# Ending a two-layer hybrid step: a third output tile beside the last recurrence, a listed order, sums on ScalarE, and a rotary product read from PSUM

## The chip, the cores and the metric

The kernel runs on one core of a Trainium2 chip. A core has a matmul engine (TensorE, PE in the profile, its weight loads PEld) and three engines that work on vectors: VectorE (DVE), ScalarE (ACT) and GpSimd (POOL); SyncE (SP) issues transfers. All work on a shared on-chip memory (SBUF); matmul results land in PSUM, eight banks of 512 fp32 columns on 128 partitions. The metric is the device time of one execution in microseconds (us), the median of several runs.

## The reference

The program is one step of a two-layer model of width 1024 on 640 tokens: 512 latent and 128 context tokens, five tiles of 128 tokens. Each layer modulates its input by an adaptive shift and scale, mixes tokens, multiplies by SiLU of a gate path, projects by an output weight, adds 4^0.25 times the residual, and normalises (LayerNorm). Layer 0 mixes by grouped-query attention with RMS-normalised queries and keys and rotary positions, layer 1 by a gated linear recurrence in both directions, eight heads of 128.

```python
q = _rms_norm(q.reshape(B, L, N_HEADS, HEAD_DIM), q_gain)     # layer 0
q = _apply_rope(q, cos, sin)          # xf * cos + rotated * sin
...
o = (o_fw + flip(o_bw)).transpose(0, 2, 1, 3)                 # layer 1
o = _rms_norm(o, norm_gain).reshape(B, L, REC_VAL_WIDTH)
gated = (o * jax.nn.silu(g.astype(jnp.float32))).astype(h.dtype)
return gated @ w_out, s_fw, s_bw
...
y = (xf - mu) * lax.rsqrt(var + LN_EPS) * g + b               # LayerNorm of x * alpha + gate * mixed
```

Outputs are both token streams, the new keys and values of the context tokens, and the final recurrent states (new_s).

## The kernel before

Each fp32 product is made of three matmuls of a shorter type: an operand is split in a high part (`hi`, a cast on ScalarE) and the rest (`lo`, a subtraction on VectorE or GpSimd), and hi x hi, hi x lo, lo x hi are added up in PSUM. The weights arrive in pieces of 512 KB (tile `raw`, SP's queue) and are split by `split_piece`.

The first half (layer 0 up to its output weights) stands in a block whose instructions a scheduler orders by an estimate of times. There, beside the attention of one group of heads (`att_gen`: scores `sc`, probabilities `p`, their transposes `pt`, and products `pot`), `q_gen` projects the queries of the next group in three units of tokens (two tiles, two tiles, one context tile): matmuls `qmm` into a bank, squares on ScalarE and their sums on VectorE, `rs_t` and a power on GpSimd (`rstd`), then on VectorE `qn` = bank x rstd, the rotary products `u` and `r` (for the context tile only the gain `qg`), the split into `qs2`, and four transposes `qps` on TensorE. Matmuls `adaps` for the adaptive gates stand between; VectorE adds them to `acc`.

The second half is written in program order. `proj_gen` projects one head (`vgps`, `rps`), 48 us each, while `gla_gen` works on the recurrence of the head before. A recurrence has seven levels: matmuls `lv` on TensorE, and products on the tile `A` on VectorE, with `kc` a copy on ScalarE. Then come transposes `kp`, their copy `kt`, the state products `sp`, six state updates and copies of the new state `ns`, the outputs `op`, squares of them on ScalarE (`ss`), `rs_t`, the power, the products with the norm and the gate (`on`), transposes `oT`, and their split `ghi`, `glo`. A `Lane` starts each stage of a recurrence when a counted time since the last is over.

The last head's recurrence has no projection beside it. `tail_gen` gives it other work: splitting the eight pieces of the output weight, and the output projection of token tiles 0 and 1 for heads 0 to 6 (slices k of the weight), 42 matmuls per tile. `weave` takes SIDE_T = 2.2 steps of it for each stage of the recurrence, and the tile framework places them. After the recurrence the five output tiles are finished one by one: the rest of the matmuls (`out_mms`, into `outp`, which has two banks), and `Norm(1, tt)`: per half `y` = outp x gate, `y` + alpha x, BN_STATS; then BN_AGGR, `rs_t`, power, and the closing pair of products with the norm's gain and bias, and the output's transfer, its halves on SP's and ScalarE's queues. Four PSUM tiles of two banks each serve all of this (`bank2`). The residual `x` comes from `x1a` by transfers on GpSimd's queue.

## Time and profile before

| | us |
|---|---|
| median of 3 runs | 873.47 (872.31 to 873.93) |
| the profiled execution | 873.58 |
| its span, first to last instruction | 871.8 |
| TensorE busy | 819.8 (94%) |
| VectorE busy | 533.8 (61%) |
| ScalarE busy | 373.0 (43%) |
| GpSimd busy | 212.9 (24%) |

The profile is of one execution. A row of its timeline has the start in us from the span's start, the length, engine, line and operation, output and inputs, the shape, and in brackets how long the engine stood idle ahead of it and which instruction ended that. Matmuls overlap, so the distance between two starts tells their cost, and a length does not. The granted clock is the share of TensorE's full clock.

### The profile page before, as it was taken

The numbers are of one execution on the slowest core, as the hardware profiler recorded it, in microseconds if no ns is written. First come the engines' busy times: TensorE is split into PE (matmuls) and PEld (weight loads), VectorE is DVE, ScalarE is ACT, GpSimd is POOL, SyncE is SP. The second block draws the span as 40 slices with busy tenths as digits, with TensorE's granted clock in tenths as the row PEclk, the third lists the DMA queues.
The fourth block names the chain that finished last, engine by engine and source line by source line (L and its number), as shares of the span: only waits on it lengthen the run. The fifth ranks groups of instructions, "written<-read, shape, count | busy, mean of one in ns | idle before, by whom it ended". The sixth has DMA issues, their size and how long they took to land.

```text
span 871.8 us, 19257 instructions
## 1 busy us (share of the span) xinstructions
PE 819.8 (94%) x8120; PEld 732.0 (84%) x8120; DVE 533.8 (61%) x952; ACT 373.0 (43%) x735; POOL 212.9 (24%) x263
## 2 busy tenths in 40 slices
PE   6999999979899988999999999999999999979794
PEld 4789998858778766888899999999999999977683
DVE  3656435735746666676437575758577576757485
ACT  2232536544655767222434444345354443453100
POOL 0213002533424644110001314042333243211010
PEclk9999999989999999999999999999999999989998
DMA  9932212162232253631223323332323232241131
GB/s 339 356 98 85 79 44 74 50 211 87 73 128 67 79 172 120 217 121 40 94 71 72 104 60 88 77 105 68 110 59 114 67 94 84 81 182 50 55 121 48
DMA packets 33991, 92.50 MB, mean 106 GB/s; under 512 B 5025, under 2 KB 12209, under 8 KB 33905
## 3 DMA queue, kind: packets, MB, share of 16 engines
q1 hardware_dynamic: 22416, 71.90, 24.5%
q0 software_dynamic: 4864, 14.44, 5.5%
q10 hardware_dynamic: 6624, 4.93, 1.9%
q8 instruction: 64, 1.05, 0.5%
q14 instruction: 23, 0.18, 0.1%
HBM read 82.06 MB, written 9.19 MB: 105 GB/s over the span
## 4 chain that ended last, share of the span: by engine, by line
PE 85%; DVE 5%; DMA 3%; ACT 3%; issue 1%; POOL 1%; SPq 0%; DVEq 0%; ACTq 0%; POOLq 0%
PE rps L1116 7%; PE rps L1117 6%; PE rps L1118 6%; PE vgps L1106 5%; PE vgps L1108 4%; PE vgps L1107 4%; PE outp L1001 4%; PE outp L1002 4%; PE outp L1003 4%; PE pot L758 3%; PE pt L840 3%; PE lv L1246 2%; PE gps L327 2%; PE gps L328 2%; PE gps L329 2%; PE sc L731 2%
## 5 line engine op out<-in xcount | busy, mean ns | idle before, releaser
L1116 PE MATMUL rps<-h1hi,rhi 128*128 128x320 f32 x368 | 117.9, 320 | 0.0
L1117 PE MATMUL rps<-h1lo,rhi 128*128 128x320 f32 x368 | 113.7, 309 | 0.0
L1118 PE MATMUL rps<-h1hi,rlo 128*128 128x320 f32 x368 | 113.5, 309 | 0.0
L833 POOL TENSOR_SCALAR p<-p,rc 128x640 f32<-128x640 f32 x64 | 54.6, 858 | 70.7 <-DVE rc L832 61.3
L1116 PEld LDWEIGHTS rps<-h1hi,rhi 128*128 128x128 f32 x368 | 69.1, 188 | 1.3
L1117 PEld LDWEIGHTS rps<-h1lo,rhi 128*128 128x128 f32 x368 | 69.2, 188 | 0.0
L1118 PEld LDWEIGHTS rps<-h1hi,rlo 128*128 128x128 f32 x368 | 69.1, 188 | 0.0
L222 DVE TENSOR_TENSOR rlo<-raw,rhi 128x1024 fp32r<-128x1024 f32 x32 | 45.0, 1410 | 33.9 <-ACT rhi L221 33.9
L1274 POOL COPY At<-near 32x160 f32<-32x160 f32 x32 | 14.0, 438 | 201.3 <-DVE near L1236 200.3
L828 ACT ACTIVATE p<-sc,nm 128x640 f32<-128x640 f32 x64 | 51.0, 798 | 24.8 <-DVE nm L825 21.0
L825 DVE TENSOR_REDUCE nm<-sc 128x1 f32<-128x640 f32 x64 | 51.8, 818 | 15.5 <-PE sc L732 15.2
L1224 ACT COPY kc<-A 128x640 f32<-128x640 f32 x40 | 32.2, 804 | 57.7 <-DVE A L1255 51.1
L221 ACT CAST rhi<-raw 128x1024 fp32r<-128x1024 f32 x32 | 33.6, 1049 | 49.9 <-PE rps L1117 47.0
L1106 PE MATMUL vgps<-rhi,h1hi 128*128 128x256 f32 x180 | 51.5, 286 | 1.2 <-ACT h1hi L956 1.2
L840 PE MATMUL pt<-small,p 128*128 128x128 f32 x320 | 50.2, 280 | 2.2 <-DVE acc L316 1.4
L1108 PE MATMUL vgps<-rhi,h1lo 128*128 128x256 f32 x180 | 50.8, 282 | 0.4 <-DVE h1lo L957 0.4
L1107 PE MATMUL vgps<-rlo,h1hi 128*128 128x256 f32 x180 | 50.6, 281 | 0.0
L736 ACT COPY pts<-pt 128x512 f32<-128x512 f32 x64 | 36.2, 589 | 32.9 <-PE pt L840 32.5
L731 PE MATMUL sc<-kk,X 128*128 128x320 f32 x128 | 42.5, 341 | 4.7 <-ACT p L828 4.2
L840 PEld LDWEIGHTS pt<-small,p 128*128 128x128 f32 x320 | 37.1, 142 | 11.2 <-issue 6.2
L1106 PE MATMUL vgps<-wspare,h1hi 128*128 128x256 f32 x140 | 41.6, 297 | 0.0
L327 PE MATMUL gps<-hhi,whi 128*128 128x320 f32 x128 | 40.0, 312 | 0.4 <-ACT X L584 0.4
(265 smaller groups left out, 2373.2 us busy)
## 6 DMA issues: line engine op xcount, KB each, us to landing
raw<-in_rec_w_in SPq DMA_DIRECT2D x40, 512.0 KB, 3.8
raw<-in_ada_s SPq DMA_DIRECT2D x32, 512.0 KB, 3.8
raw<-in_ada_m SPq DMA_DIRECT2D x16, 512.0 KB, 7.7
raw<-in_attn_w_in SPq DMA_DIRECT2D x16, 512.0 KB, 4.3
raw<-in_attn_w_out SPq DMA_DIRECT2D x8, 512.0 KB, 4.2
raw<-in_rec_w_out SPq DMA_DIRECT2D x8, 512.0 KB, 3.5
x1d<-y SPq DMA_DIRECT2D x5, 512.0 KB, 2.6
rx<-x1d POOLq DMA_DIRECT2D x20, 128.0 KB, 3.7
```

Of the source, the lines that this page charges most:

```text
L327: nc.tensor.matmul(ps[:, :320], w.hi(k)[:, c], hhi[:, k, t], start=(k == 0), stop=False)
L731: nc.tensor.matmul(out, X[:, h, t0:t0 + P], kk[:, c, k0:k1], start=True, stop=False)
L825: nc.vector.tensor_reduce(nm[:, 0:1], sc[:, :, :320], AX.XY, ALU.max, negate=True)
L828: nc.scalar.activation(halves(p[:]), sc[:, :, :320], AF.Exp, bias=nm[:, 0:1], accum_out=su[:, 0:1])
L833: nc.gpsimd.tensor_scalar(p, p, rs[:, 0:1], 1.0, ALU.mult, ALU.mult)
L840: nc.tensor.transpose(pt[:, i * 256 + q * P:i * 256 + (q + 1) * P], ps[q][:, (k0 + i) * P:(k0 + i + 1) * P], ident)
L1106: nc.tensor.matmul(out, h1hi[:, k, t], hi, start=(k == 0), stop=False)
L1107: nc.tensor.matmul(out, h1hi[:, k, t], lo, start=False, stop=False)
L1108: nc.tensor.matmul(out, h1lo[:, k, t], hi, start=False, stop=(k == KT - 1))
L1116: nc.tensor.matmul(ps[:, j, :320], hi[:, k, :], h1hi[:, k, t], start=(k == 0), stop=False)
L1117: nc.tensor.matmul(ps[:, j, :320], hi[:, k, :], h1lo[:, k, t], start=False, stop=False)
L1118: nc.tensor.matmul(ps[:, j, :320], lo[:, k, :], h1hi[:, k, t], start=False, stop=(k == KT - 1))
```

## The change

It has six parts.

1. Norm's sums on ScalarE. For layer 1, class `Norm` gives way to `Out`. For token tiles 0, 1, 3 and 2, in this order, BN_STATS and BN_AGGR go; ScalarE takes a sum of each half of `y` by a Copy with accumulation, and a sum of squares about the mean by a Square with accumulation: 16 new instructions on 128x512. VectorE works out the mean with two tiny operations (`spread`). Token tile 4, the last, keeps BN_STATS, in parts of 256 columns. Its second half is multiplied in two parts of 256 columns, 24 matmuls each.
2. Listed order. `tail_steps` gives out its steps one for each stage of the last recurrence; `weave` and `Side` are not used there. It goes on to the third output tile: slices 0 to 6 of tile 2, 42 matmuls, behind the levels, kp, sp and op.
3. Three pieces of the output weight (`wo_early`) are split during the last head's projection, one more than was there so far, into a new buffer `wx0`. Two of the five residual tiles are loaded early, the others after the last oT.
4. Gate ahead of norm: in `gla_gen`, `on` = op x g, then on x rstd, for every head. The squares' own output goes to `kt`, no longer to `on`.
5. Queries' rotary: `rope_raw` makes `u` and `r` from the bank before rstd is there, and `rms_scale` multiplies by rstd after. The count of operations is the same.
6. The transfers of four output tiles go on SP's queue alone.

```diff
@@ class Out (new), its statistics
+            for nh, s, y in todo:
+                nc.vector.scalar_tensor_tensor(y, self.x[:, s], ALPHA, y, ALU.mult, ALU.add)
+                if self.last:
+                    for i in range(s.start, s.stop, CW):
+                        nc.vector.bn_stats(self.st[:, self.n, :], self.y[:, i:i + CW])
+                        self.n += 1
+                else:
+                    j = junk.tile([P, 512], F32, tag="j", name="j")
+                    nc.scalar.activation(j, y, AF.Copy, accum_out=self.st[:, nh, 0:1])
...
+        def spread(self):
+            t = self.st
+            nc.vector.tensor_scalar(t[:, 0, 1:2], t[:, 0, 0:1], t[:, 1, 0:1], -1.0 / D, ALU.add, ALU.mult)
+            nc.vector.tensor_scalar(t[:, 0, 2:3], t[:, 0, 1:2], D ** -0.5, 0.0, ALU.mult, ALU.add)
+            for nh in range(2):
+                j = junk.tile([P, 512], F32, tag="j", name="j")
+                nc.scalar.activation(j, self.y[:, nh * 512:(nh + 1) * 512], AF.Square, bias=t[:, 0, 2:3], scale=D ** -0.5,
+                                     accum_out=t[:, 1, 1 + nh:2 + nh])
@@ q_gen
             ps = yield from tok_unit(w, tt0, n, "qmm")
             rstd = rms_stat(ps, n)
+            r = rope_raw(ps, tt0, n, cosq, sinq, qg)
             yield
...
-            qn = rms_apply(ps, n, rstd)
-            r = rope_apply(qn, tt0, n, cosq, sinq, qg)
+            qn = rms_scale(r, n, rstd)
@@ proj_gen
         for i in range(3):
             if i:
                 load_q(i)
+            if i == 2 and h == RH - 1:
+                wo_early()
@@ gla_gen
-            nc.scalar.activation(on[:, cc], opw[:, cc], AF.Square, accum_out=ss[:, c:c + 1])
+            nc.scalar.activation(kt[:, cc], opw[:, cc], AF.Square, accum_out=ss[:, c:c + 1])
+        nc.vector.tensor_tensor(on, opw[:, :NT], g, ALU.mult)
         rsqrt(rstd[:, :TT], ss[:, :TT], 1.0 / P, NORM_EPS)
...
-        nc.vector.tensor_tensor(on, on, g, ALU.mult)
+        on3 = on[:].rearrange("p (a b) -> p a b", a=TT)
+        nc.vector.tensor_tensor(on3, on3, view(rstd, 0, [[1, TT], [0, P]]), ALU.mult)
@@ the tail
+    def tail_steps():
+        slots.extend(wr.tile([P, 1024], F32R, tag=t, name=t)[:] for t in ("whi", "wlo"))
+        wo_piece(3)
         for tt in range(2):
+            out_k(tt, 0)
+        out_k(0, 1)
+        yield
...
+        for ks in ((0,), (1,), (2,), (3, 4, 5), (6,)):
+            for k in ks:
+                out_k(2, k)
+            yield
...
-    weave(lane.gens[0][0], side, SIDE_T)
-    side.finish()
+    for _ in lane.gens[0][0]:
+        next(steps, None)
+    drain(steps)
...
+    o4.half(both[0])
+    for c in (slice(0, CW), slice(CW, 512)):
+        out_mms(o4.ps, 4, 1, ghi, glo, c=c)
+        o4.half((1, c))
+    o4.rstd()
+    o4.finish()
```

How this moves instructions shows at three places. The first is TensorE's queue where the last projection ends and the last recurrence begins; `oT` is of head 6, `lv` of head 7, `wx`, `w`, `whi` and `wlo` are parts of the output weight. Before:

```order
L1118 MATMUL rps<-h1hi,rlo 128x320
L1328 MATMUL oT<-small,on 128x128 x5
L1246 MATMUL lv<-A,kc 32x32 x20
L1001 MATMUL outp<-w_9399,ghi 128x512
L1002 MATMUL outp<-w_9399,ghi 128x512
L1003 MATMUL outp<-w_9399,glo 128x512
L1001 MATMUL outp<-whi,ghi 128x512
```

And now:

```order
L1194 MATMUL rps<-h1hi,rlo 128x320
L1406 MATMUL oT<-small,on 128x128 x5
L1031 MATMUL outp<-wx_9294,ghi 128x512
L1032 MATMUL outp<-wx_9294,ghi 128x512
L1033 MATMUL outp<-wx_9294,glo 128x512
L1031 MATMUL outp<-w_9295,ghi 128x512
...
L1031 MATMUL outp<-wx_9294,ghi 128x512
L1324 MATMUL lv<-A,kc 32x32 x20
L1032 MATMUL outp<-wx_9294,ghi 128x512
```

19 matmuls of the output tiles have moved ahead of the first level.

The second place is VectorE's queue at the last norm, and at the end, the last two token tiles; the brackets name the engines or queues that an instruction waits for. Before:

```order
L186 TENSOR_SCALAR rs_t<-sso 128x5 [waits Activation_49]
L1321 TENSOR_TENSOR on<-op,rstdo 128x640 [waits Pool_49]
L1323 TENSOR_TENSOR on<-on,g 128x640 [waits DVE_49]
...
L1021 TENSOR_TENSOR y<-outp,gate_9396 128x512 [waits DMASW6_49,PE_49]
L1022 SCALAR_TENSOR_TENSOR y<-x_9854,y 128x512 [waits DMASW3_49,DVE_49]
L1023 BN_STATS st<-y 128x6 [waits DVE_49]
L1021 TENSOR_TENSOR y<-outp,gate_9396 128x512 [waits PE_49]
```

And now:

```order
L1396 TENSOR_TENSOR on<-op,g 128x640 [waits Activation_49]
L186 TENSOR_SCALAR rs_t<-sso 128x5
L1401 TENSOR_TENSOR on<-on,rstdo 128x640 [waits Pool_49]
...
L1077 TENSOR_TENSOR y<-outp,gate_9402 128x512 [waits DMASW6_49,PE_49]
L1116 SCALAR_TENSOR_TENSOR x_9848<-x_9848,rstdl,ln_9854 128x512 [waits Pool_49]
L1116 SCALAR_TENSOR_TENSOR x_9848<-x_9848,rstdl,ln_9854 128x512
L186 TENSOR_SCALAR rs_t<-st 128x1 [waits Activation_49]
L1080 SCALAR_TENSOR_TENSOR y<-x_9852,y 128x512 [waits DMASW3_49,DVE_49]
L1116 SCALAR_TENSOR_TENSOR x_9850<-x_9850,rstdl,ln_9854 128x512 [waits Pool_49]
...
L1077 TENSOR_TENSOR y<-outp,gate_9402 128x256 [waits PE_49]
```

The product with the gate has moved ahead of rs_t, and the wait for ScalarE with it; at the end the closing products of tiles 3 and 2 (`x_9848`, `x_9850`) stand between the two halves of tile 4 (`x_9852`). On TensorE, the first matmul of the second 256-column part waits for that last product.

The third place is VectorE's queue where the context tile of the second group's queries ends, near 185 us of the trace. Before:

```order
L186 TENSOR_SCALAR rs_t<-ss 128x4 [waits DVE_49]
L316 TENSOR_TENSOR acc<-acc,adaps 128x256 [waits PE_49]
L524 TENSOR_TENSOR qn<-qmm,rstd 128x256 [waits Pool_49]
L222 TENSOR_TENSOR wlo<-raw,whi 128x1024 [waits DMAHW1_49,Activation_49]
L533 TENSOR_TENSOR r<-qn,qg 128x256 [waits DVE_49]
L575 TENSOR_TENSOR qs_2105<-r,qs_2105 128x4x64 [waits Activation_49]
```

And now:

```order
L186 TENSOR_SCALAR rs_t<-ss 128x4 [waits DVE_49]
L534 TENSOR_TENSOR r<-qmm,qg 128x256
L858 RECIPROCAL rc<-su 128x1 [waits Activation_49,Pool_49]
L550 TENSOR_TENSOR qn<-r,rstd 128x256 [waits DVE_49,Pool_49]
L222 TENSOR_TENSOR wlo<-raw,whi 128x1024 [waits DMAHW1_49,Activation_49]
L601 TENSOR_TENSOR qs_2105<-qn,qs_2105 128x4x64 [waits Activation_49]
L316 TENSOR_TENSOR acc<-acc,adaps 128x256 [waits PE_49]
```

The product with the gain has moved ahead of the power, and the addition to `acc` behind the split; the subtraction `wlo` still stands ahead of the split.

## The prediction

> **What bounds the kernel now.** I read the slices first, then the windows by stage, then the waits of the last 100 us, then the timeline there. In the page's slices PE is short of full in the first slice, in a few near slice 9, and in several of the last five; the granted clock dips once near 190 us and at the end.

> ```profile
> PE   6999999979899988999999999999999999979794
> PEclk9999999989999999999999999999999999989998
> ```

> The windows price the stages: columns are the window, its length, then busy time of PE, PEld, DVE, ACT, POOL, the granted clock, DMA share and GB/s.

> ```profile
> 100.00:350.00 250.00, 232.87 (x1909) 193.68 (x1908) 141.41 (x307) 143.92 (x306) 88.26 (x97) 0.99 0.29 99
> 350.00:750.00 400.00, 398.36 (x4561) 376.77 (x4560) 261.43 (x414) 169.28 (x318) 88.88 (x124) 1.00 0.30 91
> 776.00:822.00 46.00, 35.51 (x448) 28.08 (x446) 29.01 (x47) 17.65 (x36) 4.81 (x8) 0.91 0.31 110
> 822.00:856.00 34.00, 32.22 (x135) 25.09 (x134) 28.84 (x52) 0.60 (x1) 5.05 (x6) 0.98 0.26 92
> ```

> PE is the bound: from 350 to 750 it lacks 1.6 us of 400: what only speeds other engines there is worth nothing. From 776 to 822 PE lacks 10.5 us and runs at a mean clock of 0.91. From 822 to 856 PE and DVE are both nearly full, and ACT does nothing. In the attention, 100 to 350, it lacks 17 us. The waits from 776 on:

> ```profile
> PE oT L1328 <- DVE on L1323: 6.4, 2, 5.0
> PE lv L1246 <- ACT kc L1224: 3.3, 1, 3.3
> PE outp L1001 <- DVE y L1021: 1.8, 1, 1.8
> ```

> The profiled execution took 873.58, of which the span is 871.8; 1.78 lies outside it. The median of the runs is 873.47, 0.11 lower; I count both as one. The runs lie between 872.31 and 873.93, so 0.2% (1.75 us) is what this kernel's measurement can tell from no change.

> **The change, part by part, on the time axis of before.**

> *PE filled at the start of the last recurrence.*

> ```profile
> 777.62 0.74 PE L1328 MATMUL oT<-small,on 128*128 128x128 f32 x5 [1.43 <-DVE on L1323]
> 781.62 0.76 PE L1246 MATMUL lv<-A,kc 128*32 128x32 f32 x40 [3.26 <-ACT kc L1224]
> 784.19 0.63 PE L1002 MATMUL outp<-wlo,ghi 128*128 128x512 f32 x1
> 784.62 0.63 PE L1003 MATMUL outp<-whi,glo 128*128 128x512 f32 x1
> 786.41 0.39 PE L1002 MATMUL outp<-wlo,ghi 128*128 128x512 f32 x1
> 786.64 0.40 PE L1003 MATMUL outp<-whi,glo 128*128 128x512 f32 x1
> 800.14 0.53 PE L1246 MATMUL lv<-A,kc 128*32 128x32 f32 x38
> 806.81 1.04 PE L1286 MATMUL kp<-small,A 128*128 128x128 f32 x8
> 812.02 0.38 PE L1309 MATMUL op<-v,At 128*128 128x128 f32 x2
> 820.47 1.30 PE L1328 MATMUL oT<-small,on 128*128 128x128 f32 x5 [5.01 <-DVE on L1323]
> ```

> After the idle 3.26 a 512-column matmul starts every 0.43 us until 786, then every 0.23. The changed order puts 19 of them in that gap: 778.4 + 19 x 0.23 = 782.8, so the first level starts 1.2 later than 781.62, but at full rate. Then 17, 16, 12 and 12 matmuls lie between the next levels (each level 0.5): 782.8 + 0.5 + 3.9 = 787.2, 791.4, 794.7, 798.0. Fewer follow (3, 5, 6), so there the chain between DVE and PE rules with its old spacing, 6.7 us from the fifth level (800.14) to kp (806.81): kp at 804.7, 2.1 earlier. Kp to op was 5.2 with 10 matmuls of the outputs in it and now has 18, so 8 x 0.23 more: 7.0, and op starts at 811.7, 0.3 earlier. Op also waits now for ACT's copies of the new state (three outputs are held, so one bank tile is left for kp, sp, op and oT); I put that at 0, since it lies behind the 12 matmuls that stand between the state's products and op, 2.8 us, and the two copies have DVE's six state updates ahead of them; without that cover it would be two of ScalarE's 128-column operations, 0.6 by the 0.29 of 816.68 below. From op to oT the chain of squares, power and products is as long as before:

> ```profile
> 816.68 0.29 ACT L1317 ACTIVATE on<-op 128x128 f32<-128x128 f32 x1
> 817.09 0.17 DVE L186 TENSOR_SCALAR rs_t<-sso 128x5 f32<-128x5 f32 x1 [4.41 <-ACT on L1317]
> 817.42 1.19 POOL L187 TENSOR_TENSOR rstdo<-rs_t,mhalf 128x5 f32<-128x5 f32 x1 [12.31 <-DVE rs_t L186]
> 818.64 0.82 DVE L1321 TENSOR_TENSOR on<-op,rstdo 128x640 f32<-128x640 f32 x1 [1.38 <-POOL rstdo L187]
> 819.50 0.82 DVE L1323 TENSOR_TENSOR on<-on,g 128x640 f32<-128x640 f32 x1
> 821.81 0.79 ACT L1329 ACTIVATE ghi<-oT,ngain 128x640 fp32r<-128x640 f32 x1 [4.75 <-PE oT L1328]
> ```

> *Gate ahead of norm* gains nothing: the product with the gate now carries a wait on ScalarE's squares, and rs_t is queued behind it on DVE. Of the two products of 0.82 one merely stands on the other side of rs_t and the power (817.09 to 818.64). The bounds are 0 and -0.8; I take 0, since the wait stands in the order.

> [...]

> In heads 0 to 6 PE is full and covers either.

> From op to oT it was 8.45, so oT comes at 820.1. The 18 matmuls of the third tile (4.15 us) fill PE from op's end to some 0.9 us before that, where it idled 5.01; a gap of 1.78 (below) did not halve the clock, so oT takes 0.74, not 1.30, and ghi starts at 820.9: 0.9 earlier than 821.81.

> *Fewer matmuls left.* The third tile's 42 matmuls for seven of its eight slices are done by then. What remains after ghi (821.7) is 90 of 512 columns and 48 of 256, at half of 0.23 as an estimate: 90 x 0.23 = 20.75 and 24 x 0.12 = 2.85 bring PE to the end of the first 256-column piece at 845.3. Nothing else holds PE until there: the bank of each tile that follows has been read by DVE by its start.

> *The last piece waits for DVE.* Both 256-column pieces share one bank tile, and in the order the second waits for DVE's product of the first. So DVE's queue is counted.

> ```profile
> 825.41 0.68 DVE L1022 SCALAR_TENSOR_TENSOR y<-x,y 128x512 f32<-128x512 f32 x1
> 826.01 0.68 DVE L1021 TENSOR_TENSOR y<-outp,gate 128x512 f32<-128x512 f32 x1
> 830.33 1.40 DVE L1037 SCALAR_TENSOR_TENSOR x<-y,mv,ln 128x512 f32<-128x512 f32 x2
> 831.65 1.41 DVE L1038 SCALAR_TENSOR_TENSOR x<-x,rstdl,ln 128x512 f32<-128x512 f32 x2
> 855.21 0.50 PE L1001 MATMUL outp<-whi,ghi 128*128 128x512 f32 x1 [1.78 <-DVE y L1021]
> 861.04 0.69 DVE L1021 TENSOR_TENSOR y<-outp,gate 128x512 f32<-128x512 f32 x1 [4.42 <-PE outp L1003]
> ```

> Ahead of that product stand 18 gate and residual operations at 0.60 (825.41 to 826.01), 16 of the closing pair at 0.66 (two from 830.33 to 831.65), two 256-column statistics (0.35) and 12 tiny ones (0.15): 23.9 us. From the first output, 6 matmuls after 821.7, this is 847.0 without a wait. Two waits per pair of tiles come on top: for ScalarE, four sums in a row, and for POOL's power (1.19 at 817.42). No row shows a 512-column sum on ScalarE; the nearest are

> ```profile
> L736 ACT COPY pts<-pt 128x512 f32<-128x512 f32 x64 | 36.2, 589 | 32.9 <-PE pt L840 32.5
> L1317 ACT ACTIVATION_READ_ACCUMULATOR on<-op 128x1 f32 x40 | 8.4, 211 | 0.0
> ```

> so between 0.6 and 0.8 each; I take 0.7 (packed instructions overlap a little). Followed instruction by instruction the waits add 2.6, at 0.6 each 2.2, at 0.8 each 3.0, and the product, 0.4 itself, ends at 850.0. PE idles 4.7 us ahead of the last piece, longer than the 3.26 that halved the clock for 4.4 us (781.62 to 786), so 20 of its 24 matmuls start every 0.22 and four every 0.12: 4.9 us, end 854.9; at full clock it would be 2.85. Before, from the last product (861.04) to the end of the span were 10.76 us; three of its operations now have 256 columns and cost 0.42 (row of 187.73 below) rather than 0.69: 9.95. End: 854.9 + 0.2 for the matmul to land + 9.95 = 865.05, 6.75 less than 871.8. That DVE loses eight statistics (4.8 us) is thus paid back by waits and by the order of its queue. The three later loads of x, issued after oT on POOL's queue, where only the power of each tile comes behind them, have some 9 us before their first use.

> *Early split of an output weight in the last projection*: one more DVE subtraction of 1.22 (row of 186.59 below) ahead of the second level's product of head 6.

> ```profile
> 737.19 0.83 DVE L1255 TENSOR_TENSOR A<-A,T 128x640 f32<-128x640 f32 x1 [0.41 <-issue]
> 738.88 0.83 DVE L1260 TENSOR_TENSOR A<-A,T 128x640 f32<-128x640 f32 x1 [0.87 <-ACT kc L1224]
> 740.05 0.56 PE L1246 MATMUL lv<-A,kc 128*32 128x32 f32 x40
> ```

> Idle 0.41 and the slack from 739.71 to 740.05 take 0.75 of it, or the delay propagates whole: 0.5 to 0.9. I take +0.7, PE being full there.

> *Queries' rotary from PSUM*: same count and size of operations; a DVE operation took 0.68 from PSUM (826.01) as from SBUF (825.41). Its longest wait before is here:

> ```profile
> 185.51 1.04 ACT L221 CAST whi<-raw 128x1024 fp32r<-128x1024 f32 x1 [1.91 <-DMA raw<-in_attn_w_in]
> 186.59 1.22 DVE L222 TENSOR_TENSOR wlo<-raw,whi 128x1024 fp32r<-128x1024 f32 x1 [0.77 <-ACT whi L221]
> 187.73 0.42 DVE L533 TENSOR_TENSOR r<-qn,qg 128x256 f32<-128x256 f32 x1
> 189.19 0.72 PE L582 MATMUL qps<-identr,qs 128*128 128x128 f32 x4 [4.20 <-DVE qs L575]
> ```

> Now r is ready before the power, and ScalarE's cast of qs follows its cast of whi at once; but DVE's wlo still stands ahead of the split, and it waits for the same load. The split comes at 187.8 rather than 188.62, the wait shrinks to about 3.4 and the half clock stays: -0.9. The rest of this stretch is newly ordered by the scheduler; its other waits on PE are short ones, so I take 0 with 3 to either side.

> Sum: -6.75 + 0.7 - 0.9 = -6.95: 873.58 becomes 866.6.

> **Rivals.** (1) DVE keeps pace and the last piece never waits: 845.3 + 2.85 + 0.2 + 9.95 = 858.3, less 0.2, plus 1.78: 859.9. For it speaks that DVE loses 4.8 us of statistics; against it stand the 23.9 us of queue, nine tenths of the 26.5 that PE needs for all that is left (20.75 + 2 x 2.85). (2) The wait at 189 disappears with its half clock: 4.2, and 2.0 for 4.4 us at half rate, 6.2 in place of 0.9: 861.3. Against it: the load on which wlo waits is unmoved. (3) Slower: the newly ordered attention stretch opens a hole of over 3.3 us where scores or transposes found cover; from about that length the clock halves and it costs 6.2, like the one at 189. One gives 872.8, no change; two give 879.0. Against it: in before one such hole stands among a dozen shorter waits there; for it: the order there follows a scheduler's estimate of times, and PE lacks 17 us of 250 in that stretch already. (4) A part of the change not doing what it says, gate ahead, is in the sum.

> **Numbers.** Forecast 0.65 (862 to 870.5: DVE's waits 2 us to either side, the rotary's 3); rival 1 0.09; rival 2 0.07; rival 3 0.19, of which 0.08 ends within 0.2%. Faster 0.81, same 0.08, slower 0.11. The range, 860 to 873.2, takes in the forecast, rival 2, and rival 3 with one hole; rival 3 with more and most of rival 1 stay out.

> **What would show it.** Right: no wait over 2 us on PE between 776 and 822; one of 3.5 to 6 ahead of the last 24 matmuls, released by DVE's 256-column product; DVE without long idle time in the 25 us before; DVE's gate product beginning only after the last square. Wrong: that last wait missing, or a new wait of over 3 us before 350.

## The result

The changed kernel takes 865.28 us in the median of four runs (863.82 to 866.18), the kernel before 873.7 (872.31 to 876.73) beside it: a ratio of 0.989 with a 95% interval of 0.9861 to 0.9918, 8.4 us less. In a second set it was 864.44 against 874.4, ratio 0.9881 (0.9852 to 0.991). The forecast was 866.6 with a range of 860.0 to 873.2. The profiled execution of after has a span of 862.1, 9.7 less than before's.

The slices of after, in the same two rows as before. The holes of the last slices are filled but for the very last one, which goes from 4 to 3, with a clock of 6 rather than 8.

```profile
PE   6999999989999998999999999999999999999993
PEclk9999999999999999999999999999999999999996
```

The windows of after, columns as before. The stages are the same, cut at the same instructions: attention, the projections, from head 6's oT to that of head 7 and its split, from there to the last matmul.

```profile
100.00:344.00 244.00, 231.14 (x1893) 191.08 (x1893) 140.47 (x306) 142.27 (x305) 87.33 (x96) 0.99 0.30 101
344.00:744.00 400.00, 397.72 (x4551) 376.66 (x4552) 263.11 (x413) 171.05 (x319) 90.29 (x125) 1.00 0.30 91
771.70:817.10 45.40, 41.91 (x489) 33.40 (x488) 27.52 (x46) 17.36 (x35) 5.52 (x9) 1.00 0.27 91
817.10:851.70 34.60, 30.34 (x138) 26.14 (x138) 26.15 (x52) 10.89 (x32) 4.64 (x7) 0.86 0.29 107
```

In the stage of the last recurrence PE lacked 10.5 of 46 and now 3.5 of 45.4, and the clock went from 0.91 to 1.00. In the last stage it lacks 4.3, at a clock of 0.86. The waits of PE from 730 on say which:

```profile
PE outp L1031 <- DVE y L1077: 4.3, 1, 4.3
PE oT L1406 <- DVE on L1401: 2.1, 2, 1.3
PE outp L1031 <- ACT ghi L1407: 0.9, 1, 0.9
```

The rows behind these waits, from the timelines of DVE and PE. The product with the gate (L1396) does wait for the squares (kt); oT follows the 18 matmuls after 0.77; and the last 24 matmuls wait for DVE's product of the first 256 columns, which ends 31 us after oT.

```profile
812.22 0.82 DVE L1396 TENSOR_TENSOR on<-op,g 128x640 f32<-128x640 f32 x1 [5.63 <-ACT kt L1395]
815.48 0.73 PE L1406 MATMUL oT<-small,on 128*128 128x128 f32 x5 [0.77 <-DVE on L1401]
817.10 0.50 PE L1031 MATMUL outp<-w,ghi 128*128 128x512 f32 x1 [0.89 <-ACT ghi L1407]
846.10 0.41 DVE L1077 TENSOR_TENSOR y<-outp,gate 128x256 f32<-128x256 f32 x1
846.56 0.58 PE L1031 MATMUL outp<-w,ghi 128*128 128x256 f32 x1 [4.26 <-DVE y L1077]
```

Read by this one trace, the gain would be 3.95 in the attention, 5.4 from head 6's oT to the end, and 1.4 ahead of the attention's scores (their first start is 131.34 rather than 132.74), less 1.1 in the projections. Of these four figures only the last is the kernel's own, as the runs below show. The first two hold what this one execution met, and so does the third: in the twelve other traces of changed kernels the first scores start between 131.48 and 133.09.

### The profile page after: what moved, and what is told of

Read it like the earlier page. It is cut to its first block, busy times and chain, and to the rows that moved or that the text cites. A ratio compares the mean times of both kernels' runs of the same rounds, so it can differ in the third digit from the quotient of the medians.

```text
span 862.1 us, 19366 instructions
## 1 busy us (share of the span) xinstructions
PE 818.7 (95%) x8144; PEld 734.0 (85%) x8144; DVE 530.9 (62%) x952; ACT 384.0 (45%) x767; POOL 211.8 (25%) x263
## 3 DMA queue, kind: packets, MB, share of 16 engines
q8 instruction: 64, 1.05, 0.5%
## 4 chain that ended last, share of the span: by engine, by line
PE 85%; DVE 6%; ACT 3%; DMA 2%; issue 2%; POOL 1%; ACTq 0%; DVEq 0%; POOLq 0%
PE rps L1192 7%; PE rps L1193 6%; PE rps L1194 6%; PE vgps L1182 4%; PE vgps L1184 4%; PE vgps L1183 4%; PE outp L1031 4%; PE pot L784 4%; PE outp L1032 4%; PE outp L1033 4%; PE pt L866 3%; PE lv L1324 2%; PE gps L327 2%; PE gps L328 2%; PE gps L329 2%; PE sc L757 2%
## 5 line engine op out<-in xcount | busy, mean ns | idle before, releaser
L222 DVE TENSOR_TENSOR rlo<-raw,rhi 128x1024 fp32r<-128x1024 f32 x32 | 45.4, 1421 | 33.9 <-ACT rhi L221 33.9
L221 ACT CAST rhi<-raw 128x1024 fp32r<-128x1024 f32 x32 | 33.6, 1049 | 52.0 <-PE rps L1193 48.4
```

## The experiments

Three stretches are compared: from the first of the attention's diagonal scores (`pscp`) to the first matmul of the projections (`h1t`), from there to head 6's oT, and from that oT to the end of the span. In before they take 238.32, 406.56 and 94.18.

**The rotary products alone.** Before with part 5 of the change and nothing else.

```diff
...
             rstd = rms_stat(ps, n)
+            r = rope_raw(ps, tt0, n, cosq, sinq, qg)
...
-            qn = rms_apply(ps, n, rstd)
-            r = rope_apply(qn, tt0, n, cosq, sinq, qg)
+            qn = rms_scale(r, n, rstd)
...
```

> The kernel before with the queries' rotary products from PSUM alone. The step of the prediction: the split near 189 us comes 0.9 earlier and nothing else changes, so 0.9 below the kernel before. What the two traces say: the first scores of the second, third and fourth group of heads start 4.5, 4.6 and 6.3 us earlier and the first transposes of the second half 5.4, so 5.4 below. If the tail's edits had a hand in that, the gain here is smaller than 5.4. On the wait near 189: 2.0 us as in the trace after, if the earlier load is the cause, since the order of the attention is the same here.

872.51 (868.93 to 875.04) against 874.69, ratio 0.9973 (0.9956 to 0.999): -2.2, by the interval -0.9 to -3.8. The stretch is 237.02, not the 234.4 of after's trace. The wait near 189 is 2.27 rather than 4.20, and the reason is in four rows of the trace of rot_only.

```profile
184.15 1.04 ACT L221 CAST whi<-raw 128x1024 fp32r<-128x1024 f32 x1 [1.33 <-DMA raw<-in_attn_w_in]
185.23 1.22 DVE L222 TENSOR_TENSOR wlo<-raw,whi 128x1024 fp32r<-128x1024 f32 x1 [1.77 <-ACT whi L221]
186.37 0.42 DVE L601 TENSOR_TENSOR qs<-qn,qs 128x256 fp32r<-128x256 f32 x1
186.94 0.51 PE L608 MATMUL qps<-identr,qs 128*128 128x128 f32 x4 [2.27 <-DVE qs L601]
```

DVE's queue is as forecast: wlo, and the split right behind it. But the load is earlier too. Times are counted here from the first diagonal scores, 132.74 in before and 132.00 in rot_only. The next rows are, in before and then in rot_only, the load's issue on SP's queue, the subtraction `wlo` of the piece ahead of it on DVE, and the two units of conditioning matmuls on PE, ahead of the loads and just ahead of the wait.

```profile
181.82 0.33 SPq L208 DMA_DIRECT2D raw<-in_attn_w_in  x1
...
180.57 1.23 DVE L222 TENSOR_TENSOR wlo<-raw,whi 128x1024 fp32r<-128x1024 f32 x1
...
174.02 1.07 PE L265 MATMUL adaps<-raw,sil 128*32 128x256 f32 x16
183.92 1.07 PE L265 MATMUL adaps<-raw,sil 128*32 128x256 f32 x16
```

```profile
180.46 0.33 SPq L208 DMA_DIRECT2D raw<-in_attn_w_in  x1
...
179.21 1.23 DVE L222 TENSOR_TENSOR wlo<-raw,whi 128x1024 fp32r<-128x1024 f32 x1 [1.44 <-ACT whi L221]
...
172.55 1.07 PE L265 MATMUL adaps<-raw,sil 128*32 128x256 f32 x16
183.60 1.07 PE L265 MATMUL adaps<-raw,sil 128*32 128x256 f32 x16
```

The load is issued at 48.46 after 49.08, the cast behind it starts at 52.15 after 52.77, and the transposes that PE waits for at 54.94 after 56.45. Of these 1.5, 0.6 are the load's and 0.9 those of the shorter chain behind it. The first unit of `adaps`, at 40.55 after 41.28, has eight score matmuls fewer ahead of it in the new order (52 rather than 60 from the first diagonal scores on). When its last matmul is done, the load of the piece ahead is issued (41.68 after 42.41), and when DVE has subtracted that piece, the load in question (in all fourteen traces but no_load, which lacks it, within 0.1 of that subtraction's end). The second unit is later, 51.60 after 51.18: up to the wait PE has the same 423 matmuls in both orders, but is through with them 0.4 later in the new one, where they keep it 0.8 longer with 0.35 less idle time between. So the wait is 1.9 shorter, and what is gained of it by the transposes is 1.5. In the ten other traces with this code and this load the issue lies between 48.38 and 48.49, but for second_look with 48.82; in tail_only, with the old code, it is at 49.13.

**The tail alone.** After with the old rotary code, so parts 1 to 4 and 6.

```diff
-            r = rope_raw(ps, tt0, n, cosq, sinq, qg)
...
-            qn = rms_scale(r, n, rstd)
+            qn = rms_apply(ps, n, rstd)
+            r = rope_apply(qn, tt0, n, cosq, sinq, qg)
...
```

> The changed kernel with the queries' rotary as before: all tail edits alone. The prediction's terms: -6.75 + 0.7, 6.0 below the kernel before. What the traces say: 5.4 gained from head 6's last transposes to the end, 1.1 lost to the early split in the last projection: 4.3 below. Rival: the two halves of the change hinder one another, then this and the rotary alone do not add up to the 8.4 of the whole.

867.19 (865.31 to 871.03), ratio 0.9919 (0.9888 to 0.995), -7.5 against the 874.69 beside it. Its attention takes 238.06, its projections 407.36 and its tail 86.84. So the tail as such is worth 7.3, two more than after's own trace shows, and the projections cost 0.8. With rot_only's 2.2 the two halves make 9.7, and the whole of after was 8.4 and 10.0 in its two sets: they add, within the scatter.

**A PSUM tile of its own for the last 24 matmuls.**

```diff
     for c in (slice(0, CW), slice(CW, 512)):
+        if c.start:
+            o4.ps[1] = bank2("outp")
         out_mms(o4.ps, 4, 1, ghi, glo, c=c)
```

> The changed kernel with the second 256-column part of the last half in a PSUM tile of its own. By the theory the wait of 4.3 us ahead of the last 24 matmuls falls away with its half clock, DVE's queue sets the first part's product (846.1 in the trace after) and the second follows at once, at 847.4 in place of 852.1: 4.7 below the changed kernel, near 860.6. Rival, VectorE's queue being the true bound of the whole stretch and PE only waiting along: the same product at 846.1, so the same gain; told apart by DVE's idle time before the second product, 0 by the theory. Rival, another wait takes the place (the bank of tile 2 read late): gain below 2.

859.94 (858.77 to 861.76), ratio 0.9832 (0.981 to 0.9855), 5.3 below after. Its waits of PE from 805 on are two, and the products of the two 256-column parts stand back to back on DVE:

```profile
PE outp L1031 <- ACT ghi L1407: 0.9, 1, 0.9
PE oT L1406 <- DVE on L1401: 0.8, 1, 0.8
...
846.95 0.74 DVE L1077 TENSOR_TENSOR y<-outp,gate 128x256 f32<-128x256 f32 x2
```

PE's last matmul starts at 845.50, and DVE takes the two products only from 846.95 on. So the matmuls that the change had wait for DVE had no need to: the bank tile they share set the wait, and it cost 5.1 of the stretch (82.03, against 87.14, the mean of tail_only, gate_back, late_split and second_look). With the wait gone DVE's queue sets the end.

**The last half in one piece.** The same question from the other side: no second 256-column part at all.

```diff
-    for c in (slice(0, CW), slice(CW, 512)):
-        out_mms(o4.ps, 4, 1, ghi, glo, c=c)
-        o4.half((1, c))
+    out_mms(o4.ps, 4, 1, ghi, glo)
+    o4.half(both[1])
```

> After with the last tile's second half as one piece of 512 columns instead of two of 256 in one PSUM bank. Theory (the wait ahead of the last 24 matmuls comes from the shared bank alone, and with it gone DVE's queue sets the end, whatever the size of the last piece): no wait, DVE's closing products end 0.2 to 0.5 from where own_tile's do, stretch from head 6's oT to the end 81.8 to 82.6, time 860. Rival (the 256-column pieces are worth something, since the last product, residual and statistics after the last matmul are shorter): 0.8 or more above own_tile, 861.

859.69 (858.34 to 861.68), ratio 0.9829 (0.9798 to 0.9861), stretch 82.18. The two parts of 256 columns gain nothing over one of 512, and in one bank tile they cost 5.

**Norm ahead of the gate again.**

```diff
-        nc.vector.tensor_tensor(on, opw[:, :NT], g, ALU.mult)
...
         rsqrt(rstd[:, :TT], ss[:, :TT], 1.0 / P, NORM_EPS)
...
-        nc.vector.tensor_tensor(on3, on3, view(rstd, 0, [[1, TT], [0, P]]), ALU.mult)
+        nc.vector.tensor_tensor(..., opw[:, :NT]..., view(rstd, 0, [[1, TT], [0, P]]), ALU.mult)
+        nc.vector.tensor_tensor(on, on, g, ALU.mult)
```

> The changed kernel with norm first and gate after, as before. By the prediction's step gate ahead is worth 0: within 0.4 of the changed kernel, and from the last square to the last transposes 3.3 to 3.5 us in both. Rival: gate ahead is worth one product, then this is 0.8 slower.

865.56 (864.55 to 866.54), ratio 0.9894 (0.9873 to 0.9916), and a tail of 87.04: no different from after. Its rows on DVE show the same wait of 5.62, now ahead of rs_t, and the same 1.38 for POOL's power; oT comes 8.08 after op, and 7.96 in after.

```profile
816.18 0.17 DVE L186 TENSOR_SCALAR rs_t<-sso 128x5 f32<-128x5 f32 x1 [5.62 <-ACT kt L1395]
817.73 0.82 DVE L1399 TENSOR_TENSOR on<-op,rstdo 128x640 f32<-128x640 f32 x1 [1.38 <-POOL rstdo L187]
818.59 0.82 DVE L1401 TENSOR_TENSOR on<-on,g 128x640 f32<-128x640 f32 x1
819.56 0.74 PE L1406 MATMUL oT<-small,on 128*128 128x128 f32 x5 [0.88 <-DVE on L1401]
```

**The output weight's early split put back late.** The split of `wx0` keeps its place in the program's order, behind the last level of head 6's recurrence.

```diff
-        split_piece(hi, lo, ("rec_w_out", nh, i), nc.vector)
+        if n:
+            split_piece(hi, lo, ("rec_w_out", nh, i), nc.vector)
+            return
...
+        got, raw = ahead.popleft()
...
+        pin(nc.scalar.copy(hi, raw))
+        pin(nc.vector.tensor_tensor(lo, raw, hi.bitcast(F32), ALU.subtract))
```

> After, with the split of the first output weight wx0 put back behind the last level of the recurrence's third projection head, everything else as in after. Theory (the early split's subtraction of 1.22 us stands on DVE ahead of a product that PE waits for): the stretch from h1t to head 6's oT shrinks from 407.4 to 408.3 (four kernels with the early split) to 406.6 to 406.8 (the two without), -1.0; the rest as in after: median about 864.5, 9 below before. Rival (the early split costs nothing itself, the 1.0 comes from the rest of the tail's new order in the recurrence): that stretch stays at 407.4 or more and the time at 865.3. Second rival (wx0 is then late for the third output tile): PE waits at the first outp of the third tile for the split, the stretch from head 6's oT to the end grows by what the split lacks, 1 to 2 us.

863.96 (861.17 to 865.43), ratio 0.9878 (0.9849 to 0.9908). The runs alone do not tell it from after, but the stretch does: 406.58. In the five kernels without the early split it is 406.41 to 406.80, in the nine with it 407.36 to 408.28: 1.0 apart, and no value lies between. The tail was 87.39, so nothing waits for the later split.

**Statistics on VectorE again.** All output tiles take BN_STATS and BN_AGGR, in after's order of work.

```diff
+            self.last = True
+            self.end = last
...
+                    step = CW if self.end else 512
+                    for i in range(s.start, s.stop, step):
+                        nc.vector.bn_stats(self.st[:, self.n, :], self.y[:, i:i + step])
...
         def spread(self):
+            return
```

> After, with the sums of every output tile taken by DVE's statistics again, as before, in place of ScalarE's running sums; the order of the pieces as in after. Theory (DVE's queue sets when the last 24 matmuls may start): eight statistics of 0.60 come back on DVE, +4.8, and ScalarE's waits of 2.2 to 3.0 go; the wait of PE ahead of the last 24 matmuls grows from 4.3 to 6.2 to 7.0, and the time from 865.3 to about 867.5. Rival (ScalarE's sums buy nothing, since what DVE saved was paid back by waits for them): the wait stays within 0.5 of 4.3 and the time within 1 of 865.3. Rival (ScalarE's sums are worth their whole 4.8): wait 9, time 870.

866.64 (865.57 to 869.1), ratio 0.9917 (0.9889 to 0.9945), and a tail of 89.41, 2.3 above the mean of the tails with ScalarE's sums. The wait has grown by 2.1 to 2.3:

```profile
851.83 0.58 PE L1031 MATMUL outp<-w,ghi 128*128 128x256 f32 x1 [6.60 <-DVE y L1079]
```

The sums themselves, as groups of ScalarE's lines in after from 818 to 862:

```profile
L1095 ACT ACTIVATE j<-y,st 128x512 f32<-128x512 f32 x8 | 5.7, 710 | 0.0
L1087 ACT ACTIVATE j<-y 128x512 f32<-128x512 f32 x8 | 5.0, 623 | 13.5 <-DVE y L1080 7.8 <-DMA x<-x1a 5.7
L1095 ACT ACTIVATION_READ_ACCUMULATOR j<-y,st 128x1 f32 x8 | 1.5, 188 | 0.0
```

So of the 4.8 that DVE is spared, 2.3 reach the end of the kernel. Only a small part of the rest is paid back in waits for these sums. From DVE's first product of the output tiles to that of the first 256-column part it is 27.34 us in bn_back, without idle time, and 25.25 in second_look (the unedited kernel's second execution, below), with 1.3 of idle time. These are its waits over 0.1:

```profile
830.29 0.75 DVE L1116 SCALAR_TENSOR_TENSOR x<-x,rstdl,ln 128x512 f32<-128x512 f32 x1 [0.47 <-POOL rstdl L187]
...
838.32 0.22 DVE L1091 TENSOR_SCALAR st<-st 128x1 f32<-128x1 f32 x1 [0.25 <-ACT j L1087]
...
845.04 1.42 DVE L1116 SCALAR_TENSOR_TENSOR x<-x,rstdl,ln 128x512 f32<-128x512 f32 x2 [0.44 <-POOL rstdl L187]
```

So 0.25 is waited for ScalarE and 0.91 for the power on POOL. By the distances between starts, the eight tiny operations of `spread` take 1.0, where BN_AGGR takes 0.45, and the other pieces 0.8 more than in bn_back. It is DVE's queue that the last 24 matmuls wait for: what it gets longer by comes out in that wait.

**One idle time of PE in place of two.** Six matmuls of the third output tile (`held`) are moved from ahead of head 7's oT to behind it.

```diff
             nc.tensor.transpose(wide(pt)[:, cc], on[:, cc], ident)
+        if hook:
+            hook.pop()()
...
-        for ks in ((0,), (1,), (2,), (3, 4, 5), (6,)):
...
+        hook.append(held)
+        for ks in ((0,), (1,), (2,), (3, 4, 5)):
```

> After, with the six matmuls of the third tile's seventh slice (1.4 us) moved from before oT of head 7 to behind it, so that PE has one idle time ahead of oT of about 2.2 us and none between oT and ghi, in place of two of 0.8 and 0.9. Theory (two short idle times close together lowered the clock in after's one profile only by their phase; the six matmuls cover the wait for ghi): oT at 0.74 or 0.8, matmuls from ghi on at full clock, the stretch from head 6's oT to the end 86.9 as in the other three traces of this tail; time within 0.5 of after. Rival (a single idle time of 2.2 us halves the clock as the 3.3 of before did): oT takes 1.3 and the 20 matmuls behind it start every 0.43, +3 to +4, time about 869. Rival (the two gaps cost in most executions what they cost in after's profile): -1.9 in the median, 863.4.

865.57 (861.28 to 866.59), ratio 0.9886 (0.9847 to 0.9925), tail 87.12: the time is after's, the mechanism is in part the first rival's. The first row is the single idle time. oT still takes 0.73; from 820.62 on a 512-column matmul starts every 0.43, eight of them rather than 20, and from 824.00 on every 0.23 again.

```profile
819.31 0.73 PE L1407 MATMUL oT<-small,on 128*128 128x128 f32 x5 [2.12 <-DVE on L1402]
...
821.47 0.63 PE L1512 MATMUL outp<-w,glo 128*128 128x512 f32 x1
821.90 0.63 PE L1031 MATMUL outp<-w,ghi 128*128 128x512 f32 x1
...
824.00 0.39 PE L1032 MATMUL outp<-w,ghi 128*128 128x512 f32 x1
824.23 0.39 PE L1033 MATMUL outp<-w,glo 128*128 128x512 f32 x1
```

It costs no time because the wait ahead of the last 24 matmuls shrinks with it, to 3.57, and about half of these 24 keep the full clock (starts 0.12 apart from 850.11 to 851.18, 0.21 from 851.33 on). A different order of DVE's queue also stands behind the shorter wait, so this run says only that half clock followed an idle time of 2.12.

**The changed kernel once more.**

> The changed kernel once more, nothing edited: a second profiled execution of it, for two readings that its first trace shows and the other traces of the same code do not. Theory (both belong to the one execution): the 20 matmuls behind oT of head 7 start every 0.23 and not every 0.43, so that the stretch from head 6's oT to the end is 86.9 (tail_only, gate_back, late_split) and not 88.8; the stretch from the first diagonal scores to h1t is 236 to 237 as in the other five kernels with the queries' new products, not 234.4; median 865.3. Rival (both belong to the kernel): 88.8 and 234.4 again.

864.44 (861.77 to 866.18), ratio 0.9881 (0.9852 to 0.991). The two idle times at oT and ghi are the same to 0.01, 0.76 and 0.89, and no half clock follows. These are the 3.4 us from 0.7 after the first matmul behind ghi on, in after and then in this execution (the last three numbers: granted clock, DMA share, GB/s).

```profile
817.80:821.20 3.40, 3.40 (x10) 2.71 (x9) 0.67 (x2) 0.00 (x0) 0.58 (x2) 0.52 0.95 331
```

```profile
820.10:823.50 3.40, 3.40 (x17) 2.77 (x16) 1.86 (x4) 0.00 (x0) 0.57 (x2) 1.00 0.94 323
```

Ten matmuls against seventeen. The tail is 87.27 and the attention 236.22, so after's 88.76 and 234.37 were that execution's: a half clock that cost 1.6, and a short attention.

**One load left out.** After, where the second piece of the third group's query weights is not fetched.

```diff
             src = order.popleft()
+            if src == ("attn_w_in", 2, 1):
+                ahead.append((src, ahead[-1][1]))
+                continue
```

> After without one load: the second half of the attention's query weights of the third group is not fetched, its split reads the first half's raw buffer once more (so the queries of that group are others). It is the load for which ScalarE's cast, DVE's wlo and by them PE's wait near 186 to 189 stand. Theory (the load is what is left of that wait, and the half clock behind it follows from the wait): the wait of 2.2 to 2.3 goes, with it some 2 for the half clock; first diagonal scores to h1t 236.1 becomes about 232, time 861. Rival (another load, that of the conditioning weights, or the chain of the rotary is as late): another wait of 1.5 to 2.5 at the same place, time 864 to 865. Rival (the wait goes and the clock is lowered all the same): 863.

861.01 (859.61 to 862.48), ratio 0.9844 (0.9819 to 0.987), 3.4 below the 864.44 beside it. The wait is 0.97, the clock stays full (from the row of 188.16 on the diagonal scores start 0.14 and 0.11 apart; in rot_only, at half clock, it is 0.21), and the attention takes 231.12.

```profile
186.27 0.52 PE L611 MATMUL qps<-identr,qs 128*128 128x128 f32 x4 [0.97 <-DVE qs L604]
...
188.16 0.31 PE L760 MATMUL pscp<-kk,X 128*128 128x128 f32 x1
188.30 0.27 PE L761 MATMUL pscp<-klo,X 128*128 128x128 f32 x1
188.41 0.28 PE L760 MATMUL pscp<-kk,X 128*128 128x128 f32 x1
```

The load is 1.3 of the 2.3 that were left of that wait. The kernel's order was made anew around it, and second_look has one spell of half clock in this stretch where no_load has none, so the 5.1 of the stretch is not the load's alone.

**Two edits together.** A tile of its own and the late split:

> After with both changes: a PSUM tile of its own for the second 256-column part of the last tile, and the split of wx0 put back late. Theory (the two are on the path one behind the other and add): own_tile's 859.9 less 1.0, about 858.9. Rival (late split delays the third tile's first matmuls, which now end last): 860 to 861. Rival (the two gains overlap: DVE's queue ends the kernel in both): 859.9.

859.1 (857.87 to 861.19), ratio 0.9829 (0.9802 to 0.9856). And the last half whole, with the late split:

> After with the last half whole and the split of wx0 put back late: the two edits of whole_half and late_split. Theory (they add as own_tile and late_split did): own_late's 859.1 and 0 to 0.5 either way, 858.6 to 859.6. Rival (with one piece the last product begins later than DVE is free, by what the matmuls then lack): 860 or more.

858.49 (857.87 to 860.89), ratio 0.9821 (0.9795 to 0.9846), the lowest median of all. The stretches are as in the single edits (406.41 and 82.13; 406.47 and 82.15), so they add. Between the two no difference can be told, and the second is the simpler: 15.9 below before, 6 to 7 below after.

## Why the prediction was right, and where it was not

The sum was -6.95 and the medians moved by -8.4 and -10.0. Stage by stage, with the means over all traces that share a stage:

| term | predicted | measured |
|---|---|---|
| head 6's oT to the end | -6.75 | -7.2 (94.33, mean of before and rot_only, to 87.14, mean of tail_only, gate_back, late_split, second_look) |
| early split of wx0 | +0.7 | +1.0 (406.56 to 407.57) |
| rotary from PSUM | -0.9 | -1.95 (238.19, mean of before and tail_only, to 236.24, mean of eleven); -1.3 at equal half clock (to 236.90, mean of seven) |

**The last recurrence.** From head 6's oT the prediction has the first level 5.2 later, kp 27.1, op 34.1 and oT 42.5 later; after has 4.99, 27.37, 34.18 and 42.14. The order filled the idle times, the levels after the fifth kept their spacing, and the copies of the new state held up nothing.

**Gate ahead, 0.** The wait that the order showed is in the trace (5.63 ahead of the gate's product), and gate_back measured no difference.

**The last piece waits for DVE.** From oT the prediction has the first 256-column product ended 29.9 later; it is 29.7 in second_look (847.04 + 0.41) and in tail_only (849.81 + 0.41), and 31.0 in after with its half clock. That the two agree is in part luck. The queue's work was right, 23.9 in both. But the waits on top, for ScalarE's sums and POOL's power, are 1.3 rather than 2.6, and DVE's first product begins 4.0 after oT (821.79 less 817.76 in second_look) rather than 3.0: two misses that cancel. The prediction has PE idle for 4.7 and then 4.9 of matmuls at mostly half clock; second_look has 4.48, and 5.1 from 847.50 to its last start at 852.57. The shared tile was read out of the program's order, and own_tile showed that it was the cause. ScalarE's sums were taken at 0.7; they took 0.62 and 0.71. That the statistics' 4.8 are about half paid back is what bn_back measured: 2.3 are left. Waits were to take 2.6 of it and took 1.3, most of it for POOL; tiny operations and longer pieces took the rest.

**The term that was mis-sized** is the rotary's, -0.9, where all traces together give -1.95. Its failed step is "the load on which wlo waits is unmoved". The step before it was right: wlo stands ahead of the split, waits for the load, and the chain behind the load is 0.9 shorter. But the load is issued 0.6 to 0.7 earlier (0.3 in second_look), since the scheduler's new order has the conditioning matmuls earlier that release the piece ahead of it. That these matmuls are the cause is read from the traces; no run moves them alone. The two make the 1.5 by which the transposes start earlier. The wait itself went to 2.3 and not to 3.4; 0.4 of this is only that PE comes to it later.

Of the rest, taken at 0, two things can be told apart. Both old traces hold two windows of 3.4 us at half clock in this stretch, and so do seven of the eleven new ones: from the first to these the stretch shrinks by 1.3, so behind the transposes 0.2 of the 1.5 is lost again, which is near the 0. The other 0.65 of the mean is that three of the eleven met one such window and own_late none. "The half clock stays" held near 189 in ten of the eleven, in five of them for half as long as in before (3.4 rather than 6.8 us); why it is the one or the other stays open. Rival 2, in which the wait goes whole, was not met; no_load, without this load and with an order of its own, was 3.4 faster, where the rival had 5.3.

**Rival 1** supposed that DVE keeps pace and the last piece never waits. DVE does not keep pace. With the wait taken away own_tile gained 5.1 of the stretch, where the rival had 6.7: without the wait it is DVE's queue that ends the kernel, not PE's. **Rival 3**, a new hole in the attention, did not come: in none of the eleven traces does PE wait longer than 2.4 in this stretch. Its "from about that length the clock halves", said of 3.3, is too long, though: waits of 1.78 in own_tile and 1.84 in late_split were followed by half clock. The gap of 1.78 in before was not: an edge at 854.23 of the grid that is read below parts it, and of the 3.41 us ahead of this edge and behind it PE is busy for 2.61 and 2.43.

The forecast came out 1.3 above the first median, 2.2 above the second. Both of the larger misses, 1.05 of the rotary (0.4 of it at equal half clock) and 0.45 of the tail, point the same way, the 0.3 of the split the other.

## What to carry to other kernels

Where the last work is cut in pieces so that its closing can begin sooner, give the pieces PSUM tiles of their own, or do not cut: two pieces in one tile order the second's matmuls behind the first's readout, and behind all that is queued on the reading engine ahead of it (here a wait of 4.48 us in second_look, and 5.1 of the stretch). When code is moved in a block that a scheduler orders, follow what frees the buffers of the loads beside it: here a load is issued within 0.1 us of the end of its buffer's last reader, and that reader has moved too (the issue by 0.6 in rot_only, 48.46 after 49.08). And before a difference of two traces is explained, compare the same stretch in every trace that shares its code; after's trace had 1.6 us more in the tail than the mean of four others, and 1.9 less in the attention than the mean of eleven.

## What the runs showed of the hardware

In these traces the half clock comes in pieces of one length, 3.4 us. Read in windows of a quarter of a us, the spell at the wait near 189 lasted 6.8 us in before, rot_only, gate_back, bn_back, one_gap and whole_half, 3.4 in after, second_look, tail_only, own_tile, late_split and whole_late, and did not come at all in own_late and no_load. Rows with the same wait of 2.3 to 2.4 and the same code there: own_late first, then whole_late, then, with 2.27, rot_only (the granted clock is the third number from the end).

```profile
187.40:190.80 3.40, 2.95 (x29) 2.40 (x30) 0.64 (x2) 1.66 (x3) 2.12 (x4) 1.00 1.01 369
```

```profile
187.70:191.10 3.40, 3.40 (x23) 2.26 (x21) 0.00 (x0) 1.28 (x3) 2.12 (x4) 0.52 0.70 276
```

```profile
188.00:194.80 6.80, 6.80 (x35) 5.94 (x27) 2.03 (x4) 3.43 (x13) 2.11 (x5) 0.50 0.46 166
```

That is none, one and two spells of 3.4 us after much the same wait. Each is worth up to 1.7, an estimate (half of its 3.4); the one in after's tail cost 1.6. Waits of 2.0 to 2.4 near 189, in ten of the eleven traces with the queries' new products and this load, the single one of 2.12 in one_gap, and, in one of the eleven traces with such a pair, two of 0.77 and 0.89 with 0.73 of work between them, were followed by half clock. So were these two, in own_tile and in late_split:

```profile
328.18 1.07 PE L866 MATMUL pt<-small,p 128*128 128x128 f32 x8 [1.78 <-ACT pts L762]
```

```profile
317.95 1.08 PE L265 MATMUL adaps<-raw,sil 128*32 128x256 f32 x8 [1.84 <-DMA raw<-in_ada_s]
```

What differs is where an edge of the grid parts an idle time. In rot_only the wait of 2.27 lies in one step (184.57 to 187.98, PE busy 1.14 of 3.41 us). In own_late an edge at 186.26 parts the 2.33, the two steps have 2.68 and 1.82 busy, and the clock stays full. The pair of 0.77 and 0.89 lies in one step in after (814.51 to 817.92, 1.76 busy); in second_look an edge at 818.56 parts it, 2.58 and 2.60 are busy, and no half clock follows. Why one wait brings one spell or two stays open, and the first 15 us do not keep to these counts. For a reader of two traces: a stretch in which PE idles for some 1.7 us within 3.4 can differ between executions of one kernel, as the tail of after and second_look did by 1.5 (88.76 and 87.27); by the estimate above, one spell makes up to 1.7 and two up to 3.4.
